# An encoder trunk in split fp32: all high products of a slot ahead of its low products, and the low parts of every fourth MLP tile made elsewhere

## The chip, the cores and the metric

The kernel runs on one NeuronCore of one Trainium2 chip. The metric is the device time of one execution in microseconds (us). Its matmuls run on TensorE (PE in the profile; its weight loads are PEld), element-wise work on VectorE (DVE) and ScalarE (ACT), a few small operations on GpSimd (POOL), and SyncE (SP) issues the transfers.

## The reference, cut to what matters

Two layers work on 256 tokens of width 2048, all in float32. Each layer is a mixer (differential attention, gated linear attention and retention heads behind one input projection and one output projection), followed by a gated MLP with a depthwise convolution of width 3:

```
h = rmsnorm(x, ln1);  x = x + mixer(h) @ w_o            # mixer: h @ w_in, heads, head norms
h = rmsnorm(x, ln2);  u = h @ w_up                       # w_up: 2048 x 11264
u = conv3(u) + conv_b;  a, g = split(u)
x = x + (a * silu(g)) @ w_down                           # w_down: 5632 x 2048
```

The output is a last rmsnorm of x, 256 x 2048.

## The kernel before, in words

A float32 product is made of three products of rounded parts. Each operand is cut into a high part, rounded to the format fp32r that TensorE reads, and a low part, the rest. Then high times high, low times high and high times low are summed in one accumulator, and low times low is dropped.

The weights come as 402 **slots**, in the order in which they are used (`slot_list`): the input projection, the 16 slots of `wo`, and then for each of three chunks of the MLP (14, 15 and 15 column blocks) alternating slots `upg` and `upa`, and 16 slots `down`. Most slots are one tile of 128 x 2048 elements, 1 MB, that is 16 blocks of 128 x 128; a `down` slot has 14 or 15 blocks.

For each slot there are three tiles from one pool of ten (`wts`, 128 x 2048 each): the raw weights that SP loads (`load`, L151), their high part (`split_hi`, L176, one ACT copy that rounds) and their low part (`split_lo`, L184, one DVE subtraction raw minus high). When slot s comes up, the program first gives out `split_hi(s + 3)` and `split_lo(s + 2)`, then the matmuls of slot s, then `load(s + 5)`. The raw tile goes back to the pool when its low part is made. The pool gives out tiles as they were given back, so the next user of a buffer waits for the last reader of its former tile.

The activations lie as tiles of 128 x 512 (`big`): 256 columns high part, 256 columns low part of the same 256 tokens. The slots of the kinds `gv`, `rv` and `dv` take the activations as TensorE's weights (`mm_token`, L222 to L224, three matmuls of 512 columns for a pair of blocks), `ga` has 64 weight columns (L212). All others, 368 slots, go through `mm_feature`: for each block j one matmul of the high weights with all 512 columns (L206), which gives high times high and high times low side by side in one PSUM bank, and one of the low weights with the high 256 columns (L208), which is added to the second half of the bank:

```
for first in ((True, False) if k < n - 1 else (False, True)):
    if first:
        pe.matmul(pt, lhsT=R(hi[:, w]), rhs=R(a), start=k == 0, stop=k == n - 1)
    else:
        pe.matmul(pt[:, T:], lhsT=R(lo[:, w]), rhs=R(a[:, :T]), start=False, stop=False)
```

So a slot is a row of pairs, high then low, and the last pair is turned round.

Behind the matmuls of an `up` slot its bank is read out (`gather`: ACT L229 copies one half, DVE L230 adds the other, L236 multiplies by the norm), convolved (ACT L805, DVE L806 and L807), and for `upg` put through silu (ACT L814). For `upa` it is multiplied by the gate (DVE L817) and cut into parts (ACT L819, DVE L820). A `down` slot adds its bank to the stream x (DVE L894). Every engine works through its own list in the order in which the program gave the work out and waits at each instruction for the semaphores that it needs. POOL has little to do: the power of minus one half in the norms (L320, L358) and some memsets (L254, L466, L467).

Of the kernel before, what the change touches and what calls it, by code (L numbers as in the profile page):

```python
# [14 lines left out]
AF = mybir.ActivationFunctionType  # L15
ALU = mybir.AluOpType
# [4 lines left out]
P = 128  # L21
T = 256
# [30 lines left out]
def slot_list():  # L53

    out = []
    for l in range(DEPTH):
        for kind, i in in_proj_order():
            out.append((l, kind, i, 0, 512 if kind == "ga" else 2048))
        for o in range(KB):
            out.append((l, "wo", o, 0, 2048))  # L60
        j0 = 0
        for c, n in enumerate(CHUNKS):
            for j in range(j0, j0 + n):
                out.append((l, "upg", j, c, 2048))
                out.append((l, "upa", j, c, 2048))
            for o in range(KB):
                out.append((l, "down", o, c, n * P))
            j0 += n
    return out
# [30 lines left out]
def encoder_kernel(ctx: ExitStack, tc: tile.TileContext, wflat, xT, par, con, masks, gate_w, lam_p, rel_bias, decay, out):  # L100
    nc = tc.nc
    pe, act, dve, pool = nc.tensor, nc.scalar, nc.vector, nc.gpsimd
# [30 lines left out]
    def R(ap):  # L133
        return ap.bitcast(F32R)
# [4 lines left out]
    slots = slot_list()  # L139
# [13 lines left out]
    def parts(s):  # L153

        n = slots[s][4]
        if slots[s][1] == "ga":
            h = his[s][:, :1024].rearrange("p (k c) -> p k c", c=64)
            return raws[s][:, :512].rearrange("p (k c) -> p k c", c=32), h[:, :, :32], h[:, :, 32:]
        return raws[s][:, :n], his[s][:, :n], los[s][:, :n] if s in los else None

    def split_piece(s, q):
# [6 lines left out]
        if q == 3:  # L168
            wts.put(raws.pop(s))

    def split_hi(s):
        if s >= NS or s in his:
            return
        his[s] = wts.get()
        raw, hi, _ = parts(s)
        act.activation(R(hi), raw, AF.Copy)  # L176

    def split_lo(s):
        if s >= NS or s not in raws or s not in his:
            return  # L180
        if slots[s][1] != "ga":
            los[s] = wts.get()
        raw, hi, lo = parts(s)
        dve.tensor_sub(R(lo), raw, hi)  # L184
        wts.put(raws.pop(s))

    def done(s):
# [7 lines left out]
    def mm_feature(s, pt, acts, order=None):  # L195

        hi, lo = his[s], los[s]
        n = len(acts)
        for k, j in enumerate(order or range(n)):
            a = acts[j]  # L200
            if k == n // 2 and middle:
                middle.pop()()
            w = slice(j * P, (j + 1) * P)
            for first in ((True, False) if k < n - 1 else (False, True)):
                if first:
                    pe.matmul(pt, lhsT=R(hi[:, w]), rhs=R(a), start=k == 0, stop=k == n - 1)  # L206
                else:
                    pe.matmul(pt[:, T:], lhsT=R(lo[:, w]), rhs=R(a[:, :T]), start=False, stop=False)  # L208

    def mm_ga(s, pt, acts):  # L210
        for k, a in enumerate(acts):
# [653 lines left out]
    first = [banks.get(), banks.get()]  # L865
    for k in range(KB):
        s = k // 4
        norm.operand(k)
        split_piece(s, k % 4)
        mm_token(s, first, norm.acts, [k])  # L870
        if k % 4 == 3:
            done(s)
            load(s + 5)
        if k == 13:
            split_hi(4)
            split_lo(4)
# [52 lines left out]
    for s in range(4, NS + 1):  # L929
# [39 lines left out]
        for t in (1, 2, 3):  # L969
            split_hi(s + t)  # L970
        for t in (1, 2):
            split_lo(s + t)
# [144 lines left out]
```

## Time and profile before

| what | value |
|---|---|
| median of 3 runs | 2334.39 us (2334.32 to 2334.72) |
| the profiled execution's own time | 2334.08 us |
| its span, first to last instruction | 2332.3 us |
| PE busy | 2315.1 us, 99% of the span |
| DVE busy | 1704.8 us, 73% |
| ACT busy | 1231.6 us, 53% |
| POOL busy | 62.3 us, 3% |
| transfers | 423.10 MB, mean 181 GB/s |

Matmuls overlap each other in the pipeline, so the duration of one (398 ns for 512 columns) is longer than the step from its start to the start of the next. What a matmul costs is this step.

### The profile page before, as it was taken

Reading aid. Unit: us, or ns where it says so; the run is one execution under the profiler, and the core shown is the slowest. Engines: PE = TensorE matmul, PEld = TensorE weight load, DVE = VectorE, ACT = ScalarE, POOL = GpSimd, SP = SyncE. Lnnn points to the kernel's source line nnn. Section 1 sums busy time; section 2 is a strip of 40 time slices with the busy share of each in tenths; the row PEclk is TensorE's granted clock in tenths of the full one; section 3 lists DMA queues with packets and bytes.
Section 4 is the critical chain, followed back from the end, with each engine's and each line's share of the span. In section 5 each row is a group of like instructions: output and inputs, shape, how many; then the busy total and the mean of one; then the engine's idle time right before and its main releaser. Section 6 shows DMA issues by size and latency. Waiting matters only on the chain.

```text
span 2332.3 us, 32603 instructions
## 1 busy us (share of the span) xinstructions
PE 2315.1 (99%) x13250; PEld 2004.0 (86%) x13250; DVE 1704.8 (73%) x2459; ACT 1231.6 (53%) x1769; POOL 62.3 (3%) x77
## 2 busy tenths in 40 slices
PE   8999999999999999999999999999999999999998
PEld 7888888888888888888888888888888888888887
DVE  7978886777577765777669789767775777567764
ACT  6557654555345533555445666545543555345553
POOL 0001100000000000000000111000000000000000
PEclk9999999999999999999999999999999999999999
DMA  7444455555555555555554444555545554555552
GB/s 291 167 173 162 161 176 191 180 182 171 196 193 186 190 186 187 191 181 187 185 183 172 145 163 153 193 181 181 187 177 196 185 194 175 187 198 181 186 180 104
DMA packets 66645, 423.10 MB, mean 181 GB/s; under 512 B 7960, under 2 KB 10904, under 8 KB 28096
## 3 DMA queue, kind: packets, MB, share of 16 engines
q1 hardware_dynamic: 66352, 420.96, 51.3%
q8 instruction: 104, 1.70, 0.3%
q14 instruction: 45, 0.37, 0.0%
q10 hardware_dynamic: 144, 0.06, 0.0%
HBM read 417.83 MB, written 2.11 MB: 180 GB/s over the span
## 4 chain that ended last, share of the span: by engine, by line
PE 98%; DVE 2%; DMA 0%; ACT 0%; issue 0%; ACTq 0%; SPq 0%; DVEq 0%
PE bank L206 58%; PE bank L208 29%; PE bank L222 2%; PE bank L223 2%; PE bank L224 2%; PE bank L683 1%; DVE wts L184 0%; PE bank L543 0%; PE bank L265 0%; PE bank L266 0%; DVE big L528 0%; PE bank L212 0%; PE bank L623 0%; PE bank L672 0%; DVE big L568 0%; DMA wts<-wflat 0%
## 5 line engine op out<-in xcount | busy, mean ns | idle before, releaser
L206 PE MATMUL bank<-big,wts 128*128 128x512 f32 x5760 | 2016.8, 398 | 0.0
L208 PE MATMUL bank<-big,wts 128*128 128x256 f32 x5760 | 1556.6, 281 | 0.0
L206 PEld LDWEIGHTS bank<-big,wts 128*128 128x128 f32 x5760 | 1061.4, 188 | 231.6 <-PE bank L591 0.9
L208 PEld LDWEIGHTS bank<-big,wts 128*128 128x128 f32 x5760 | 1087.4, 189 | 32.6
L176 ACT ACTIVATE wts<-wts 128x2048 fp32r<-128x2048 f32 (+3 forms) x398 | 744.1, 1871 | 366.6 <-PE bank L208 348.6
L184 DVE TENSOR_TENSOR wts<-wts,wts 128x2048 fp32r<-128x2048 f32 (+3 forms) x398 | 888.4, 2233 | 12.3 <-PE bank L223 8.2
L894 DVE TENSOR_TENSOR x<-bank,x 128x256 f32<-128x256 f32 x256 | 108.7, 425 | 244.7 <-PE bank L206 240.3
L230 DVE TENSOR_TENSOR sml<-sml,bank 128x256 f32<-128x256 f32 (+1 forms) x242 | 101.6, 420 | 213.6 <-ACT sml L229 213.4
L229 ACT ACTIVATE sml<-bank 128x256 f32<-128x256 f32 (+1 forms) x242 | 92.0, 381 | 168.5 <-PE bank L206 168.2
L819 ACT ACTIVATE big<-sml 128x256 fp32r<-128x256 f32 x88 | 36.8, 418 | 190.5 <-DVE sml L817 190.5
L814 ACT ACTIVATE sml<-sml 128x256 f32<-128x256 f32 x88 | 36.8, 418 | 158.8 <-DVE sml L807 158.8
L222 PE MATMUL bank<-wts,big 128*128 128x512 f32 x256 | 103.0, 402 | 6.0 <-ACT wts L166 6.0
L805 ACT ACTIVATE sml<-sml,conv_t 128x256 f32<-128x256 f32 x176 | 103.8, 590 | 5.7 <-DVE sml L236 5.7
L236 DVE TENSOR_TENSOR sml<-sml,sml 128x256 f32<-128x256 f32 (+1 forms) x230 | 97.8, 425 | 7.9
L223 PE MATMUL bank<-wts,big 128*128 128x512 f32 x256 | 100.8, 394 | 0.0
L224 PE MATMUL bank<-wts,big 128*128 128x512 f32 x256 | 100.5, 393 | 0.0
L806 DVE SCALAR_TENSOR_TENSOR sml<-sml,conv_t,sml 128x255 f32<-128x255 f32 x176 | 84.2, 478 | 8.7 <-ACT sml L805 8.7
L807 DVE SCALAR_TENSOR_TENSOR sml<-sml,conv_t,sml 128x255 f32<-128x255 f32 x176 | 85.2, 484 | 6.3
L820 DVE TENSOR_TENSOR big<-sml,big 128x256 fp32r<-128x256 f32 x88 | 37.4, 425 | 42.6 <-ACT big L819 42.6
L222 PEld LDWEIGHTS bank<-wts,big 128*128 128x128 f32 x256 | 48.6, 190 | 17.2 <-ACT wts L166 6.0
L224 PEld LDWEIGHTS bank<-wts,big 128*128 128x128 f32 x256 | 48.5, 190 | 10.4
L223 PEld LDWEIGHTS bank<-wts,big 128*128 128x128 f32 x256 | 48.6, 190 | 9.8 <-DVE wts L167 0.4
(147 smaller groups left out, 1018.0 us busy)
## 6 DMA issues: line engine op xcount, KB each, us to landing
wts<-wflat SPq DMA_DIRECT2D x300, 1024.0 KB, 4.8
wts<-wflat SPq DMA_DIRECT2D x64, 960.0 KB, 4.7
wts<-wflat SPq DMA_DIRECT2D x32, 896.0 KB, 4.6
wts<-wflat SPq DMA_DIRECT2D x18, 256.0 KB, 5.5
x<-xT SPq DMA_DIRECT2D x8, 256.0 KB, 5.5
out<-big SPq DMA_DIRECT2D x8, 256.0 KB, 3.8
strips<-dr SPq DMA_DIRECT2D x1, 1536.0 KB, 8.6
sml<-sml SPq DMA_DIRECT2D x32, 32.0 KB, 1.9
```

Source lines behind the costliest of these rows:

```text
L176: act.activation(R(hi), raw, AF.Copy)
L184: dve.tensor_sub(R(lo), raw, hi)
L206: pe.matmul(pt, lhsT=R(hi[:, w]), rhs=R(a), start=k == 0, stop=k == n - 1)
L208: pe.matmul(pt[:, T:], lhsT=R(lo[:, w]), rhs=R(a[:, :T]), start=False, stop=False)
L222: pe.matmul(pts[tb], lhsT=al, rhs=R(hi[:, w]), start=k == 0, stop=False)
L223: pe.matmul(pts[tb], lhsT=ah, rhs=R(lo[:, w]), start=False, stop=False)
L224: pe.matmul(pts[tb], lhsT=ah, rhs=R(hi[:, w]), start=False, stop=k == KB - 1)
L229: act.activation(t[:m], pts[0][:m, T:], AF.Copy)
L230: dve.tensor_add(d[:m], t[:m], pts[0][:m, :T])
L236: dve.tensor_mul(d[:m], d[:m], rb[:m])
L805: act.activation(c, us, AF.Identity, scale=w[1], bias=w[3])
L894: dve.tensor_add(xb[i], pts[0][:, h * T:(h + 1) * T], xb[i])
```

## The change

In `mm_feature` the matmuls of one slot are put in another order: first the high weights of all its blocks, then the low weights of all its blocks. Their number and shapes are the same. The matmul that the norm puts into the middle of a slot (`middle`) stays in the middle of the high ones.

Of the MLP's slots (`upg`, `upa`, `down`) those with a number divisible by four get their low part from another engine: 34 slots in each layer, 22 of them `up` and 12 of them `down`. In layer 0 GpSimd subtracts. In layer 1 ACT writes minus the raw tile, rounded, which is minus the high part, and a transfer that GpSimd issues adds the raw tile to it where it lies.

```diff
+    def lo_by(s):
+
+        if slots[s][1] in ("upa", "upg", "down") and s % 4 == 0:
+            return ("pool", "dma")[slots[s][0]]
+        return "dve"
+
...
     def split_lo(s):
         if s >= NS or s not in raws or s not in his:
             return
+        by = lo_by(s)
         if slots[s][1] != "ga":
             los[s] = wts.get()
         raw, hi, lo = parts(s)
-        dve.tensor_sub(R(lo), raw, hi)
+        if by == "dma":
+            act.activation(R(lo), raw, AF.Copy, scale=-1.0)
+            pool.dma_start(R(lo), raw, accum_op=ALU.add)
+        elif by == "pool":
+            pool.tensor_tensor(R(lo), raw, hi, ALU.subtract)
+        else:
+            dve.tensor_sub(R(lo), raw, hi)
         wts.put(raws.pop(s))
...
-            a = acts[j]
             if k == n // 2 and middle:
                 middle.pop()()
-            w = slice(j * P, (j + 1) * P)
-            for first in ((True, False) if k < n - 1 else (False, True)):
-                if first:
-                    pe.matmul(pt, lhsT=R(hi[:, w]), rhs=R(a), start=k == 0, stop=k == n - 1)
-                else:
-                    pe.matmul(pt[:, T:], lhsT=R(lo[:, w]), rhs=R(a[:, :T]), start=False, stop=False)
+            pe.matmul(pt, lhsT=R(hi[:, j * P:(j + 1) * P]), rhs=R(acts[j]), start=k == 0, stop=False)
+        for k, j in enumerate(order or range(n)):
+            pe.matmul(pt[:, T:], lhsT=R(lo[:, j * P:(j + 1) * P]), rhs=R(acts[j][:, :T]), start=False, stop=k == n - 1)
```

PE in layer 1 before, the end of the matmuls of slot 288 (an `upg` slot) and the start of slot 289: `bank` is the accumulator, then come the activations of a block and the weight tile (15276 and 15327 are the high and the low part of slot 288, 15325 and 15379 those of slot 289). What stands in brackets are the semaphores that the instruction waits for, by the engine that raises them (DMAHW: transfers that SP issues, DMASW: transfers that POOL issues).

```order
L206 MATMUL bank_15438<-big_14215,wts_15276 128x512
L208 MATMUL bank_15438<-big_14215,wts_15327 128x256
L206 MATMUL bank_15438<-big_14262,wts_15276 128x512
L208 MATMUL bank_15438<-big_14262,wts_15327 128x256
L208 MATMUL bank_15438<-big_14304,wts_15327 128x256
L206 MATMUL bank_15438<-big_14304,wts_15276 128x512
L206 MATMUL bank_15487<-big_13604,wts_15325 128x512 [waits PE_49,Activation_49]
L208 MATMUL bank_15487<-big_13604,wts_15379 128x256 [waits DVE_49]
L206 MATMUL bank_15487<-big_13651,wts_15325 128x512
L208 MATMUL bank_15487<-big_13651,wts_15379 128x256
```

And now, where the low part of slot 288 is tile 15332 and its high part 15281:

```order
L215 MATMUL bank_15444<-big_14215,wts_15281 128x512
L215 MATMUL bank_15444<-big_14262,wts_15281 128x512
L215 MATMUL bank_15444<-big_14304,wts_15281 128x512
L217 MATMUL bank_15444<-big_13604,wts_15332 128x256 [waits DMASW5_49]
L217 MATMUL bank_15444<-big_13651,wts_15332 128x256
L217 MATMUL bank_15444<-big_13698,wts_15332 128x256
```

The pairs are gone: the 16 low products stand in a row behind the 16 high ones, and the first low product waits for the transfer that made the low tile, where before a low product waited for DVE.

ACT in layer 1 before, about the high part of slot 289 (L176 into 15325): L229 reads out a bank, L805 and L819 belong to the convolution and the gate.

```order
L229 ACTIVATE sml_15321<-bank_15285 128x256 [waits PE_49]
L176 ACTIVATE wts_15325<-wts_15269 128x2048 [waits DMAHW7_49]
L805 ACTIVATE sml_15329<-sml_15320,conv_t 128x256 [waits DVE_49]
L819 ACTIVATE big_15334<-sml_15329 128x256 [waits DVE_49]
L229 ACTIVATE sml_15373<-bank_15337 128x256 [waits PE_49]
L176 ACTIVATE wts_15377<-wts_15318 128x2048 [waits DMAHW0_49]
```

And now:

```order
L238 ACTIVATE sml_15326<-bank_15290 128x256 [waits PE_49]
L182 ACTIVATE wts_15330<-wts_15274 128x2048 [waits DMAHW7_49]
L192 ACTIVATE wts_15332<-wts_15222 128x2048
L814 ACTIVATE sml_15335<-sml_15325,conv_t 128x256 [waits DVE_49]
L828 ACTIVATE big_15340<-sml_15335 128x256 [waits DVE_49]
L238 ACTIVATE sml_15379<-bank_15343 128x256 [waits PE_49]
L182 ACTIVATE wts_15383<-wts_15323 128x2048 [waits DMAHW0_49]
```

A second copy of a whole weight tile (L192, into the low tile of slot 288) stands behind the high part of slot 289 and ahead of the convolution's first step. POOL's transfer onto this tile waits for it.

DVE in layer 0 before, about a slot whose number is divisible by four: L230 and L236 read out a bank, L184 makes a low part (4976 is that slot's), L806 and L807 are the convolution.

```order
L230 TENSOR_TENSOR sml_4969<-sml_4970,bank_4934 128x256 [waits Activation_49]
L236 TENSOR_TENSOR sml_4969<-sml_4969,sml_4180 128x256 [waits DVE_49]
L184 TENSOR_TENSOR wts_4976<-wts_4866,wts_4922 128x2048 [waits DMAHW6_49]
L806 SCALAR_TENSOR_TENSOR sml_4978<-sml_4969,conv_t,sml_4978 128x255 [waits Activation_49]
L807 SCALAR_TENSOR_TENSOR sml_4978<-sml_4969,conv_t,sml_4978 128x255 [waits DVE_49]
L230 TENSOR_TENSOR sml_5018<-sml_5019,bank_4983 128x256 [waits Activation_49]
L236 TENSOR_TENSOR sml_5018<-sml_5018,sml_4180 128x256 [waits DVE_49]
L184 TENSOR_TENSOR wts_5025<-wts_4915,wts_4974 128x2048 [waits DMAHW7_49]
```

And now:

```order
L239 TENSOR_TENSOR sml_4969<-sml_4970,bank_4934 128x256 [waits Activation_49]
L245 TENSOR_TENSOR sml_4969<-sml_4969,sml_4172 128x256 [waits DVE_49]
L815 SCALAR_TENSOR_TENSOR sml_4978<-sml_4969,conv_t,sml_4978 128x255 [waits Activation_49]
L816 SCALAR_TENSOR_TENSOR sml_4978<-sml_4969,conv_t,sml_4978 128x255 [waits DVE_49]
L239 TENSOR_TENSOR sml_5018<-sml_5019,bank_4983 128x256 [waits Activation_49]
L245 TENSOR_TENSOR sml_5018<-sml_5018,sml_4172 128x256 [waits DVE_49]
L197 TENSOR_TENSOR wts_5025<-wts_4915,wts_4974 128x2048 [waits DMAHW7_49,PE_49]
```

The subtraction of tile 4976 has left DVE's list; it is an instruction of POOL now (L195), and the next slot's subtraction (5025) stands where it stood.

## Rows read from the trace of the kernel before

**Rows 1.** The page: busy time of each engine; granted clock of TensorE in 40 slices

```profile
PE 2315.1 (99%) x13250; PEld 2004.0 (86%) x13250; DVE 1704.8 (73%) x2459; ACT 1231.6 (53%) x1769; POOL 62.3 (3%) x77
...
PEclk9999999999999999999999999999999999999999
```

**Rows 2.** The chain that ended last: shares of the span by line

```profile
by line: PE bank L206 57.8%; PE bank L208 29.3%; PE bank L222 2.2%; PE bank L223 2.1%; PE bank L224 2.1%; PE bank L683 0.6%; DVE wts L184 0.5%; PE bank L543 0.5%; PE bank L265 0.4%; PE bank L266 0.4%; DVE big L528 0.3%; PE bank L212 0.3%; P
```

**Rows 3.** Groups by line and shape: xcount | busy us, mean ns | idle before

```profile
L206 PE MATMUL bank<-big,wts 128*128 128x512 f32 x5760 | 2016.8, 398 | 0.0
```

**Rows 4.** The same chain in order of time: start us, us, what

```profile
999.78 0.47 PE bank L206 x2
1000.25 0.11 PE bank L208
1000.36 0.23 PE bank L206
1000.59 0.12 PE bank L208
...
1005.43 0.47 PE bank L206 x2
```

**Rows 5.** Timeline of PE, token slots of 512 columns: start us, us, line, xcount

```profile
12.67 0.39 PE L222 MATMUL bank<-wts,big 128*128 128x512 f32 x1
...
28.99 0.39 PE L222 MATMUL bank<-wts,big 128*128 128x512 f32 x1
...
99.17 0.39 PE L223 MATMUL bank<-wts,big 128*128 128x512 f32 x1
...
100.33 0.39 PE L222 MATMUL bank<-wts,big 128*128 128x512 f32 x1
```

**Rows 6.** Timeline of PE, a run of 256-column matmuls (L265, L266)

```profile
165.66 0.28 PE L265 MATMUL bank<-big,big 128*128 128x256 f32 x1
...
168.52 0.40 PE L206 MATMUL bank<-big,wts 128*128 128x512 f32 x1
```

**Rows 7.** Chain in order of time, the slot with 64 weight columns

```profile
30.51 3.68 PE bank L212 x16
```

**Rows 8.** Timelines of PE and ACT about a slot's end

```profile
1027.88 0.63 PE L206 MATMUL bank<-big,wts 128*128 128x512 f32 x2
...
1028.32 0.38 ACT L229 ACTIVATE sml<-bank 128x256 f32<-128x256 f32 x1 [0.33 <-PE bank L206]
1028.60 1.91 ACT L176 ACTIVATE wts<-wts 128x2048 fp32r<-128x2048 f32 x1
```

**Rows 9.** Timeline of DVE in an up slot

```profile
1023.08 0.42 DVE L230 TENSOR_TENSOR sml<-sml,bank 128x256 f32<-128x256 f32 x1 [1.65 <-ACT sml L229]
1023.53 0.43 DVE L236 TENSOR_TENSOR sml<-sml,sml 128x256 f32<-128x256 f32 x1
1023.88 2.28 DVE L184 TENSOR_TENSOR wts<-wts,wts 128x2048 fp32r<-128x2048 f32 x1
1026.08 0.48 DVE L806 SCALAR_TENSOR_TENSOR sml<-sml,conv_t,sml 128x255 f32<-128x255 f32 x1
1026.59 0.48 DVE L807 SCALAR_TENSOR_TENSOR sml<-sml,conv_t,sml 128x255 f32<-128x255 f32 x1
```

**Rows 10.** Loads: median us from issue to landing; the queue's share of 16 engines (page)

```profile
q1 hardware_dynamic: 66352, 420.96, 51.3%
...
wts<-wflat SPq DMA_DIRECT2D x300, 1024.0 KB, 4.8
```

**Rows 11.** Timelines of DVE and POOL about GpSimd's power in the norms (L358, L320)

```profile
237.63 2.29 DVE L184 TENSOR_TENSOR wts<-wts,wts 128x2048 fp32r<-128x2048 f32 x1
237.87 2.60 POOL L358 TENSOR_TENSOR tny<-tny,mhalf 128x2 f32<-128x2 f32 x1 [18.80 <-DVE tny L357]
...
424.20 0.70 POOL L320 TENSOR_TENSOR tny<-tny,mhalf 128x2 f32<-128x2 f32 x1 [104.25 <-DVE tny L317]
```

**Rows 12.** Groups of POOL: a memset over 512 columns

```profile
L467 POOL MEMSET big<- 128x512 f32 x2 | 1.1, 530 | 0.0
```

## The prediction

> **What bounds the kernel now.** I read the busy times first: PE is busy for 2315.1 us, 99% of the span, and its granted clock stands at the top of the scale in all 40 slices, the higher of its two levels, 2.4 GHz [rows 1]. Next the chain of waits by line: the two lines of the feature slots hold 57.8% and 29.3% of the span, and no other engine comes to one per cent on any line [rows 2]. So whatever makes these matmuls start closer together is time won, and what the other engines do costs nothing until PE has to wait. The 87.1% are 0.871 x 2332.3 = 2031.4 us for 5760 pairs of a high and a low matmul [rows 3], which is 352.7 ns a pair. The chain in order of time shows the pair in its steps: 0.23 us for a high product of 512 columns, 0.11 or 0.12 us for a low one of 256, and 0.47 us for the two high ones that meet where two slots border [rows 4].
>
> **The order of the products.** Nothing is added or removed on PE; the question is what a matmul costs behind one of its own kind. High behind high: the token slots are long rows of 512-column matmuls, each with its own load of 128 weight columns, as the high products will be. Three lines share a row of 72 steps there, from 12.67 to 28.99 us, which is 226.7 ns a step [rows 5]. After a break the row does not start at this pace: five steps from 99.17 to 100.33 take 232 ns each, so I add 5 x 5.3 = 27 ns per slot. Low behind low: 24 steps of 256-column matmuls lie between 165.66 and 168.52, 119.2 ns each [rows 6]. A pair then costs 226.7 + 119.2 = 345.9 ns, and the sum is 5760 x 345.9 = 1992.4 us, plus 368 slots x 27 ns = 9.9 us, 2002.3 us in all. Against 2031.4 us that is 29 us less. I take -29 us.
>
> The bounds, from the nearest rows: the best is 226.7 with the low product's steps of now, 0.115 us as the mean of 0.11 and 0.12 [rows 4], and no slow start: 341.7 x 5760 = 1968.2, -63 us. In the middle is the one slot with 64 weight columns, where 16 matmuls of 512 columns take 3.68 us, 230 ns each [rows 7]; with 119.2 this is 349.2 ns, -20 us. The worst is the two high products at the border, 235 ns each [rows 4]; with 119.2 this is 354.2 ns a pair, +9 us. I take the token slots because they are the longest row with the same shape, and the border pair has a low product just ahead of it, as the first steps of a new row have.
>
> A full slot now takes (1005.43 - 999.78) = 5.65 us [rows 4] and then 16 x 345.9 + 27 = 5.56 us. Can the others follow? DVE has 0.42 + 0.43 + 2.28 + 2 x 0.48 = 4.1 us of work in an `upg` slot [rows 9] and two operations of about 0.43 more in an `upa` slot, 4.95. Both are under 5.56, so DVE does not become the bound.
>
> **GpSimd's low parts, layer 0.** 34 subtractions leave DVE and stand on POOL. No row has a POOL subtraction of 2048 columns. Below: a memset of 512 columns takes 530 ns [rows 12], so one pass over 2048 takes 2.1 us. Above: two reads and a write as three such passes, 6.4 us. I take the upper end. The subtraction can start when the buffer of its output is free, at the end of the slot three before its own, and the low products of its own slot begin after two whole slots and the high row of the third: 2 x 5.56 + 16 x 0.2267 + 0.03 = 14.8 us later. So even 6.4 us is hidden, with 8 us to spare. The raw tile is freed at 6.4 instead of about 3.5 us, and the load that takes its buffer, 4.8 us long [rows 10], ends near 11.2 us; ACT wants it for a high part only at two slots, 11.1 us, and PE at five, 27.8 us. Cost 0; if the cover were gone, 34 x the excess over 14.8 us.
>
> There is a second price: POOL and DVE get in each other's way. GpSimd's power in the norms takes 0.70 us alone, but 2.60 us when it starts under DVE's subtraction of two weight tiles, which runs from 237.63 to 239.92, and it ends 0.55 us after it [rows 11]: POOL stood still until DVE was done. The Trainium skill (SBUF — State Buffer, Who interferes with whom) says that a VectorE instruction with two SBUF inputs and a GpSimd instruction that reads SBUF exclude each other for the whole instruction; the trace agrees for POOL as the one that waits, 2.60 against 0.70 us. So DVE may now stand still while POOL subtracts, and behind its L236 wait the convolution, the next read-out and the next low part. Four `up` slots hold 2 x 4.1 + 2 x 4.95 - 2.28 = 15.8 us of DVE work. DVE's first instruction with two SBUF inputs in a slot is L236 at 1023.53 [rows 9], 1.1 us after the slot's start (1028.12 less 5.65), so up to 5.3 of POOL's 6.4 us block it: 21.1 us, under 4 x 5.56 = 22.2. Cost 0.
>
> **The accumulating transfers, layer 1.** 34 DVE subtractions become an ACT copy and a transfer on POOL's queue each. ACT has room (53% busy [rows 1]). The time that counts is from the copy to the low products. ACT reads out the bank 0.20 us after a slot's first matmul (1028.32; the second high product in the row at 1027.88 starts the slot at 1028.12), makes a high part from 0.48 to 2.39 us, and then the negated copy, of the same length, to about 4.25 us [rows 8]. From there to the low products at 14.8 us are 10.5 us. In the 12 `down` slots no read-out stands ahead of the copy, and 11 to 12 us remain for a somewhat smaller tile.
>
> How long the transfer takes no row shows. Below: like a load, 4.8 us from issue to landing [rows 10]. A load's share of the wire is 51.3% x 2332.3 us x 1.049 MB / 420.96 MB = 3.0 us [rows 10], so 1.8 us are fixed. The accumulation reads two tiles, so 1.8 + 2 x 3.0 = 7.8 us, and one load is on the way beside it in every slot; if half of it falls into the transfer, 9.3 us. Above: two reads and a write that follow each other, with the whole load, 1.8 + 4 x 3.0 = 13.8 us. I take 9.3 us, which is covered with 1.2 us to spare: cost 0. This is the thinnest cover of the change. Past 10.5 us PE stands still at the first low product of each of these slots, with the whole of PE's list behind it; SP's load into the same raw buffer would be late too, but it has until five slots on. DVE and ACT wait for such transfers too where they take over a buffer, mostly one of an earlier slot; a copy that waits on ACT holds the read-outs behind it, which PE misses only when its banks run out. The norm's power of layer 1 stands behind the first transfer on POOL; that is one wait.
>
> **The sum.** Against the execution's own 2334.08 us: -29 + 0 + 0 gives 2305 us. The median of the runs, 2334.39, stands 0.3 us above it, so I keep 2305.
>
> **The rivals.** A, the transfer is late. At 13.8 us PE would wait 3.3 us in 22 `up` slots and about 1 us in 12 `down` slots, 85 us: 2305 + 85 = 2390 us, slower. It decides from 10.5 us on, and eats the whole gain at 10.5 + 29 / 22 = 11.8 us. For it speaks that nothing in the trace shows a transfer that adds, and that the margin is a tenth; against it that only half of the wire is in use. Chance 0.32, a third of it between 10.5 and 11.8 us and so still faster.
>
> B, POOL and DVE block each other longer than I counted. If POOL's subtraction takes 8 us, DVE loses 6.9 us in four slots and needs 22.7 against 22.2: 0.5 us x 22 = 11 us, 2316 us. The long cover to 14.8 us speaks against more. Chance 0.04.
>
> C, the order buys nothing: the high row keeps the border's 235 ns, and the time is between 2334 and 2343 us. For it speaks that a step's length seems to hang on what goes before: the 64-column slot stays at 230 ns and does not settle. [...] Chance 0.12.
>
> The forecast has 0.52. Its own range is 2271 (the best bound) to 2314 us (the 64-column pace). For the range of 8 in 10 I go up to 2400, above A at its price, with one in ten left beyond (a transfer that handles its packets one by one), and down to 2275. About 0.2%, 4.7 us, is what a measurement of this kernel can tell from no change. Faster: the forecast, a third of A and B, less a little where these shade into no change, 0.63. Same: that, and the near end of C, 0.06. Slower: the rest of A and of C, 0.31.
>
> **What would show it.** Right: in the chain of waits steps of 0.227 us in the high rows and 0.12 us in the low rows, up slots of 5.56 us, PE with no idle time before L217, transfers of tile onto tile landing within 10.5 us, and POOL subtractions under 8 us, with the read-out's second instruction on DVE (L236 now, L245 then) as their victim, PE untouched. Wrong: a wait of PE's L217 on a transfer in every fourth slot of layer 1, against none in layer 0, is A; high steps of 235 ns are C; PE waiting for POOL in layer 0 is B.

## The result, and the profile after

| kernel | median of the runs, us | ratio to before, 95% interval |
|---|---|---|
| before, same chip | 2334.55 (2334.32 to 2334.96) | |
| changed | 2401.79 (2398.77 to 2403.34) | 1.0286 [1.0268, 1.0304] |

The changed kernel is slower by 67.2 us, where 2305 us were predicted. The profiled execution has a span of 2399.3 us. The page of the changed kernel, against [rows 1]: busy time, and the two rows of 40 slices for PE and for its granted clock.

```profile
PE 2313.5 (96%) x13250; PEld 2026.9 (84%) x13250; DVE 1663.7 (69%) x2391; ACT 1279.3 (53%) x1803; POOL 258.2 (11%) x145
...
PE   8999999998999989998999999999999898999997
...
PEclk9999999998999989999999999999999999999999
```

PE now has slices below nine tenths, and its share fell from 99% to 96%. The chain of waits by engine (by line it stood in [rows 2] before):

```profile
PE 65%; DVE 18%; DMA 7%; ACT 5%; issue 4%; POOL 1%; ACTq 0%; POOLq 0%; SPq 0%; DVEq 0%
```

Before, the same view gave PE 98% and DVE 2%; now DVE holds 18% and transfers 7%. Yet the matmuls themselves have the pace that was predicted. PE in an undisturbed stretch of layer 0 (start us, us, line, count), against [rows 4 to 6]:

```profile
523.15 3.82 PE L215 MATMUL bank<-big,wts 128*128 128x512 f32 x16
526.80 2.08 PE L217 MATMUL bank<-big,wts 128*128 128x256 f32 x16
528.72 3.82 PE L215 MATMUL bank<-big,wts 128*128 128x512 f32 x16
...
545.42 3.82 PE L215 MATMUL bank<-big,wts 128*128 128x512 f32 x16
```

From start to start the high row takes 3.65 us, 228 ns a step, the low row 1.92 us, 120 ns a step, and the slot 5.57 us; 5.56 were predicted. Over the whole trace the median step is 227 ns behind a high product and 120 ns behind a low one. So the loss is nowhere in the rows. It stands in few places, and the first two of these rows name two kinds of them, while the last two are waits of DVE and ACT (engine, line, what it waited for: us in all, times, longest):

```profile
PE bank L215 <- DVE big L829: 42.4, 9, 8.0
PE bank L217 <- DMA wts<-wts: 19.8, 7, 8.2
DVE wts L197 <- DMA wts<-wts: 92.4, 15, 9.6
ACT big L828 <- DVE sml L826: 249.7, 88, 6.6
```

The first kind is a wait of a high product for the last MLP activation (L829). It falls on the first `down` slot of a chunk, here in layer 0:

```profile
578.82 2.91 PE L215 MATMUL bank<-big,wts 128*128 128x512 f32 x12
585.48 0.50 PE L215 MATMUL bank<-big,wts 128*128 128x512 f32 x1 [3.75 <-DVE big L829]
593.86 0.80 PE L215 MATMUL bank<-big,wts 128*128 128x512 f32 x1 [7.87 <-DVE big L829]
594.45 3.19 PE L217 MATMUL bank<-big,wts 128*128 128x256 f32 x14
597.44 2.91 PE L215 MATMUL bank<-big,wts 128*128 128x512 f32 x7
```

The slot takes 18.6 us from 578.82 to 597.44, where before a slot of 14 blocks took 4.94. The second kind is a wait of a low product for a transfer, in layer 1. Behind either, TensorE's clock is low for a while (the stretches of PE in us from:to, its length, busy time and count of each engine, the granted clock, the DMA share and GB/s; 0.50 is 1.2 GHz, 1.00 is 2.4 GHz):

```profile
1884.70:1888.20 3.50, 3.50 (x18) 2.84 (x16) 1.88 (x5) 2.73 (x4) 0.00 (x0) 1.00 1.02 272
1888.40:1896.60 8.20, 0.12 (x1) 0.00 (x0) 0.00 (x0) 0.05 (x1) 0.00 (x0) 0.81 0.96 268
1896.70:1900.30 3.60, 3.57 (x16) 3.57 (x17) 3.17 (x3) 0.28 (x1) 0.00 (x0) 0.50 0.02 7
```

The 16 low products behind an 8.2 us stall take 3.6 us in place of 1.92.

Of the transfers and of GpSimd the page says this (issues: count, KB each, median us to landing; the queue: packets, MB, share; the group of L195: busy us, mean ns):

```profile
q0 software_dynamic: 4896, 34.61, 7.3%
...
L195 POOL TENSOR_TENSOR wts<-wts,wts 128x2048 fp32r<-128x2048 f32 (+2 forms) x34 | 166.4, 4895 | 599.8 <-ACT wts L182 340.2
...
wts<-wts POOLq DMA_DIRECT2D x22, 1024.0 KB, 8.7
```

Both are inside the bounds of the prediction, 2.1 to 6.4 us and 4.8 to 13.8 us, and below the values taken (6.4 and 9.3).

**The lag.** A number used below is the lag of the last activation: the end of L829 of an `upa` slot, less the start of the next slot on PE. Before, it is 9.4 us at the first slot of layer 0's MLP, falls by 1.2, 1.2 and 1.0 us, and then stays at 5.98 us, but for the last two `upa` slots of a chunk; the last one has 4.54 us. After, in the first chunk of layer 0, it goes 9.3, 12.5, 10.7, 14.0, 12.2, 15.5 and so on to 20.0 us: 1.5 us more with every four slots. Where it comes from is in the rows of POOL and DVE in that stretch:

```profile
521.16 5.70 POOL L195 TENSOR_TENSOR wts<-wts,wts 128x2048 fp32r<-128x2048 f32 x1 [18.07 <-ACT wts L182]
544.93 5.71 POOL L195 TENSOR_TENSOR wts<-wts,wts 128x2048 fp32r<-128x2048 f32 x1 [18.07 <-ACT wts L182]
```
```profile
543.88 2.28 DVE L197 TENSOR_TENSOR wts<-wts,wts 128x2048 fp32r<-128x2048 f32 x1
546.09 4.83 DVE L815 SCALAR_TENSOR_TENSOR sml<-sml,conv_t,sml 128x255 f32<-128x255 f32 x1
550.96 0.48 DVE L816 SCALAR_TENSOR_TENSOR sml<-sml,conv_t,sml 128x255 f32<-128x255 f32 x1
```

POOL's subtraction starts under DVE's low part, and then DVE's convolution step, 0.48 us in [rows 9], lasts 4.83 us, until POOL is done at 550.64. Two subtractions of POOL, four slots apart, lie 23.77 us apart; PE does four slots in 22.27 (523.15 to 545.42 above). The difference is the 1.5 us. Between the two, DVE waits for ACT five times, 3.95 us in all:

```profile
528.61 0.43 DVE L829 TENSOR_TENSOR big<-sml,big 128x256 fp32r<-128x256 f32 x1 [0.48 <-ACT big L828]
...
531.17 0.48 DVE L815 SCALAR_TENSOR_TENSOR sml<-sml,conv_t,sml 128x255 f32<-128x255 f32 x1 [1.35 <-ACT sml L814]
...
532.99 0.42 DVE L239 TENSOR_TENSOR sml<-sml,bank 128x256 f32<-128x256 f32 x1 [0.82 <-ACT sml L238]
...
537.93 0.42 DVE L829 TENSOR_TENSOR big<-sml,big 128x256 fp32r<-128x256 f32 x1 [0.48 <-ACT big L828]
...
543.09 0.42 DVE L239 TENSOR_TENSOR sml<-sml,bank 128x256 f32<-128x256 f32 x1 [0.82 <-ACT sml L238]
```

### The profile page after: what moved, and what is told of

Read it like the earlier page. It is cut to its first block, busy times and chain, and to the rows that moved or that the text cites. A ratio compares the mean times of both kernels' runs of the same rounds, so it can differ in the third digit from the quotient of the medians.

```text
span 2399.3 us, 32990 instructions
## 1 busy us (share of the span) xinstructions
PE 2313.5 (96%) x13250; PEld 2026.9 (84%) x13250; DVE 1663.7 (69%) x2391; ACT 1279.3 (53%) x1803; POOL 258.2 (11%) x145
## 4 chain that ended last, share of the span: by engine, by line
PE 65%; DVE 18%; DMA 7%; ACT 5%; issue 4%; POOL 1%; ACTq 0%; POOLq 0%; SPq 0%; DVEq 0%
PE bank L215 37%; PE bank L217 20%; DVE wts L197 7%; DMA wts<-wts 5%; DVE sml L815 3%; DMA wts<-wflat 2%; PE bank L231 2%; PE bank L232 2%; PE bank L233 2%; DVE sml L816 1%; ACT wts L182 1%; DVE sml L239 1%; POOL tny L367 1%; DVE sml L245 1%; ACT sml L238 1%
## 5 line engine op out<-in xcount | busy, mean ns | idle before, releaser
L215 PE MATMUL bank<-big,wts 128*128 128x512 f32 x5760 | 1392.3, 394 | 43.0 <-DVE big L829 42.4
L215 PEld LDWEIGHTS bank<-big,wts 128*128 128x128 f32 x5760 | 1063.8, 189 | 254.4 <-DVE big L829 46.1
L197 DVE TENSOR_TENSOR wts<-wts,wts 128x2048 fp32r<-128x2048 f32 (+3 forms) x330 | 737.8, 2237 | 126.1 <-DMA wts<-wts 92.4
L217 PEld LDWEIGHTS bank<-big,wts 128*128 128x128 f32 x5760 | 749.2, 194 | 51.9 <-DMA wts<-wts 24.0
L217 PE MATMUL bank<-big,wts 128*128 128x256 f32 x5760 | 759.8, 286 | 19.9 <-DMA wts<-wts 19.8
L195 POOL TENSOR_TENSOR wts<-wts,wts 128x2048 fp32r<-128x2048 f32 (+2 forms) x34 | 166.4, 4895 | 599.8 <-ACT wts L182 340.2
L815 DVE SCALAR_TENSOR_TENSOR sml<-sml,conv_t,sml 128x255 f32<-128x255 f32 x176 | 145.1, 824 | 100.9 <-ACT sml L814 100.9
L239 DVE TENSOR_TENSOR sml<-sml,bank 128x256 f32<-128x256 f32 (+1 forms) x242 | 101.2, 418 | 122.1 <-ACT sml L238 121.7
L193 POOL DMA_DIRECT2D wts<-wts x34 | 29.5, 867 | 831.0 <-ACT wts L192 684.2
L245 DVE TENSOR_TENSOR sml<-sml,sml 128x256 f32<-128x256 f32 (+1 forms) x230 | 105.3, 458 | 7.9
L816 DVE SCALAR_TENSOR_TENSOR sml<-sml,conv_t,sml 128x255 f32<-128x255 f32 x176 | 89.4, 508 | 6.3
L367 POOL TENSOR_TENSOR tny<-tny,mhalf 128x2 f32<-128x2 f32 (+1 forms) x24 | 44.5, 1852 | 445.6 <-DVE tny L366 424.3
L829 DVE TENSOR_TENSOR big<-sml,big 128x256 fp32r<-128x256 f32 x88 | 46.0, 523 | 42.6 <-ACT big L828 42.6
```

The lines of the kernel that those rows point to most:

```text
L195: pool.tensor_tensor(R(lo), raw, hi, ALU.subtract)
L215: pe.matmul(pt, lhsT=R(hi[:, j * P:(j + 1) * P]), rhs=R(acts[j]), start=k == 0, stop=False)
L217: pe.matmul(pt[:, T:], lhsT=R(lo[:, j * P:(j + 1) * P]), rhs=R(acts[j][:, :T]), start=False, stop=k == n - 1)
L239: dve.tensor_add(d[:m], t[:m], pts[0][:m, :T])
L245: dve.tensor_mul(d[:m], d[:m], rb[:m])
L815: dve.scalar_tensor_tensor(c[:, 1:], us[:, :T - 1], w[0], c[:, 1:], ALU.mult, ALU.add)
```

## The experiments

Theory 1: the order gains about 0.09 us a slot; GpSimd sets the chain of DVE and ACT back by keeping DVE from its operands; the bill comes when a chunk's first `down` slot wants the last activation. Theory 2, for layer 1: a transfer holds its raw tile until it has landed, about 8.5 us, another slot's tile takes over that buffer, and DVE, which waits for it, holds up ACT and with it the next transfers. The rivals stand with each run.

**The order alone.** `lo_by` returns "dve" for every slot.

> High products ahead of low ones, every low part back on DVE. Theory 1 (the order gains, the two unloadings lose): undisturbed slots of the changed kernel took 0.087 us less than before, 368 x 0.087 = 32 us; the first down slot of each of six chunks gives back 1.8 us (11 us), since the last MLP activations are now wanted 1.8 us earlier, and a few slots of the mixers give back about 4. So about 2317 us, and the last MLP activation stays within 8 us behind its slot's end in both layers. Rival (it is the new order that makes PE run into late activations, the unloadings only happen beside it): the stalls of 12 to 14 us at the first down slot of a chunk stay, and the time is 2345 us or more.

Measured: 2320.41 us, ratio 0.9941 [0.9925, 0.9958], 13.4 us under before. Undisturbed slots of 16 blocks went from 5.653 to 5.567 us, those of 14 from 4.94 to 4.87. Of the 58 slots of 15 blocks that are not the first of a chunk, half gained 0.08 us and half 0.01; nearly all of the latter took 5.21 or 5.22 us already before. The first `down` slot of each of the six chunks is 1.44 or 1.67 us longer, 9.1 us in all; PE in the same slot as above:

```profile
573.30 3.14 PE L215 MATMUL bank<-big,wts 128*128 128x512 f32 x13
577.90 0.50 PE L215 MATMUL bank<-big,wts 128*128 128x512 f32 x1 [1.46 <-DVE big L829]
578.23 1.84 PE L217 MATMUL bank<-big,wts 128*128 128x256 f32 x14
```

The lag is 5.99 us in both layers, as before. Theory 1 holds; of the stalls that the rival blamed on the order, about a tenth is the order's.

**The order with GpSimd's part, and the order with the transfers.**

```
return ("pool", "dve")[slots[s][0]]     # order_pool
return ("dve", "dma")[slots[s][0]]      # order_dma
```

> The new order with GpSimd's 34 low parts in layer 0, layer 1's low parts all on DVE. Theory 1: the norm's spread and the first down slots of layer 0 cost what they cost in the changed kernel, 6 + 3 x 12 = 42 us above the order alone: about 2359 us, all of it before 1230 us. Rival (a price of the transfers of layer 1 only, or of the order): within 5 us of the order alone.

> The new order with the 34 accumulating transfers of layer 1, layer 0's low parts all on DVE. Theory 1: layer 1 loses what it lost in the changed kernel, 32 us of loss over before plus its 14 us of gain by order less the first slots' price, about 40 us above the order alone: about 2357 us, all of it after 1600 us, at four or five places of 5 to 10 us and not in every fourth slot. Rival (the transfer itself is too slow): a wait of PE at the first low product of nearly every one of the 34 slots.

Measured: 2363.26 us (1.0126 [1.0111, 1.0141]) and 2358.28 us (1.0106 [1.0091, 1.0121]). Against the order alone GpSimd costs 42.9 us and the transfers 37.9, and -13.4 + 42.9 + 37.9 = 67.4 us is the whole of the change's 67.2. With GpSimd the loss is one norm slot (6.5 us, where DVE's spread of the norm, L335, meets POOL's first subtraction: in the changed kernel its two instructions take 4.73 us there, 0.48 under the order alone) and the three first `down` slots with the slot behind each (13.0, 13.1 and 10.8 us); no other slot of layer 0 differs by 0.3 us. With the transfers, three slots hold 7.2, 8.7 and 7.2 us of it, one 3.5 and a few others 0.6 to 1.6 each; most of the 34 slots have no wait. The third of them is a chunk's first `down` slot, where PE waits 6.8 us for the last activation: in layer 1, too, part of the bill is a lag. So it is not the rival, a transfer that is too long everywhere.

**Both parts under the old order.** `mm_feature` as before.

> The old alternating order with both unloadings as in the change. Theory 1: the unloadings cost nearly the same under either order; slots of 5.65 us give the evacuation chain 0.35 us more in four slots and the last activations are wanted 1.8 us later, so the first down slots of layer 0 cost about 8 us instead of 12: 2334 + 6 + 3 x 8 + 37 = about 2400 us. Rival (the unloadings are harmless under the old order, and only the new order's earlier need of high products makes them late): 2334 to 2345 us.

Measured: 2496.22 us, ratio 1.0705 [1.0682, 1.0727]. Theory 1 said about 2400 and the rival 2345 at most: a miss. Slot by slot, the profiled execution (span 2505.1 us) lost only 16.8 us in layer 0 against before, and 155.5 in layer 1. In layer 1 (line L193 of that kernel: who waited for its transfers, us and times):

```profile
  DVE wts L197: 183.8, 28
  PEld bank L221: 126.3, 33
  PE bank L221: 112.1, 32
```

Nearly every transfer is late here: the old order wants the first low product 0.23 us into its slot, the new one behind the high row, 3.65 us into it. That the new order gives the transfers 3.4 us of cover was in none of my sums as a part of its own. In layer 0 the lag grew only in the first chunk (1.16 us per four slots); in the others it rose from 6 or 7.5 us and settled between 8.2 and 10.9, four old slots being 22.61 us long. The two parts of the change are thus not independent of its order, and rival A, a wait of PE at nearly every transfer, came true under the old order.

**GpSimd writes without reading; GpSimd subtracts in quarters.** Both from order_pool; the first leaves the low parts' contribution out:

```
-            pool.tensor_tensor(R(lo), raw, hi, ALU.subtract)
+            for h in range(2):                                   # pool_memset
+                pool.memset(lo, 0.0)
+            for a in range(0, slots[s][4], slots[s][4] // 4):    # pool_quarters
+                c = slice(a, a + slots[s][4] // 4)
+                pool.tensor_tensor(R(lo[:, c]), raw[:, c], hi[:, c], ALU.subtract)
```

> As order_pool (new order, 34 tiles of layer 0 by GpSimd), but GpSimd writes each of these low parts by two memsets of the whole tile and reads nothing (these low parts are zero, their contribution is left out). From a memset of 512 columns at 0.53 us this is about 4.2 us of GpSimd per tile, near the 4.9 us of the subtraction. Theory 1 (the subtraction excludes DVE's instructions with two SBUF operands while it runs): without reading, DVE's convolution steps stay at 0.48 us, the lag of the last MLP activation stays at 6.0 us, and the time is that of the order alone, 2320 us. Rival (any GpSimd access of that length slows DVE, or GpSimd's part simply comes late): 2355 to 2365 us, the lag growing to 15 us and more.

> As order_pool, with GpSimd's subtraction cut into four of a quarter of the tile, about 1.2 us each. Theory 1 (DVE waits for the end of one GpSimd instruction, up to 4.4 us now): a DVE instruction waits at most about 1.2 us, three of them meet GpSimd's pieces in one subtraction, so DVE loses 2 to 3.6 us in four slots instead of 4.4; the lag grows by 0 to 0.8 us per four slots instead of 1.5, and the time is 2322 to 2345 us. Rival (the lock is not handed over between GpSimd's pieces): as order_pool, 2363 us.

Measured: 2321.86 us (0.9950 [0.9933, 0.9967]) and 2322.85 us (0.9952 [0.9937, 0.9967]). DVE's first convolution step in order_pool, pool_memset and pool_quarters, with POOL's rows for the full tiles in the last two (count, busy us, mean ns, idle):

```profile
L815 DVE SCALAR_TENSOR_TENSOR sml<-sml,conv_t,sml 128x255 f32<-128x255 f32 x176 | 145.1, 824 | 33.8 <-ACT sml L814 33.8
```
```profile
L816 DVE SCALAR_TENSOR_TENSOR sml<-sml,conv_t,sml 128x255 f32<-128x255 f32 x176 | 84.5, 480 | 37.7 <-ACT sml L815 37.7
L196 POOL MEMSET wts<- 128x2048 f32 x44 | 79.6, 1809 | 387.4 <-PE bank L216 366.5 <-PE bank L218 19.6
```
```profile
L197 POOL TENSOR_TENSOR wts<-wts,wts 128x512 fp32r<-128x512 f32 x88 | 123.1, 1430 | 350.0 <-PE bank L219 330.8 <-DVE wts L199 19.3
...
L817 DVE SCALAR_TENSOR_TENSOR sml<-sml,conv_t,sml 128x255 f32<-128x255 f32 x176 | 86.4, 491 | 28.3 <-ACT sml L816 28.3
```

Two memsets, 3.6 us a tile, leave DVE at 480 ns and the lag at 5.98 us: what holds DVE is not GpSimd's work but its reading. The Trainium skill (SBUF — State Buffer, Who interferes with whom) says so: a VectorE instruction with two SBUF inputs meets a GpSimd instruction that reads SBUF, not one that only writes it. Here the trace agrees, 824 against 480 ns. So does the read-out's first instruction in order_pool (L239, one operand in a PSUM bank and one in SBUF), which takes 419 ns on the mean, against 420 under the order alone. The quarters take POOL longer in all, 4 x 1.43 = 5.7 us, and yet cost 2.4 us in place of 42.9: the lag falls back to 5.99 us by the tenth `upa` slot and stays there, since a DVE instruction waits for a quarter and not for the whole. The time is near the low end of what was expected.

**GpSimd in every eighth slot.** `s % 8 == 0` in order_pool.

> As order_pool, with GpSimd's part in every eighth slot of layer 0 instead of every fourth (17 tiles, half as many). Theory 1 (each subtraction sets the chain of DVE and ACT back by about 3.6 us, and a slot without one lets it catch up by 0.52 us, as the lag falls at a chunk's start from 9.3 over 8.3 and 7.2 to 6.2 us in two slots each): eight slots give back 4.2 us, so the lag does not grow, and what is left is at most 2 us at each first down slot: 2321 to 2327 us. Rival (a price for each subtraction): half of what order_pool lost, 2341 us.

Measured: 2320.86 us, ratio 0.9944 [0.9928, 0.9961]. This is a little under the expected range. Half of the subtractions cost 0.5 us, not half of 42.9. The lag goes 7.6, 6.5, 6.0, 6.0 in each eight slots of the second and third chunk. The price is one of a chain that does or does not catch up, as theory 1 has it.

**The transfer adds the high part; the copy goes first; the transfer goes one slot early.** All from order_dma, with the edits cut to their lines; the first leaves the low parts' contribution out:

```
-            pool.dma_start(R(lo), raw, accum_op=ALU.add)
+            pool.dma_start(R(lo), R(hi), accum_op=ALU.add)       # dma_from_hi
+        if lo_by(s + 2) == "dma": split_lo(s + 2)                # dma_first: ahead of split_hi(s + 1..3)
+        if lo_by(s + 3) == "dma": split_lo(s + 3)                # dma_early: behind them
```

> As order_dma (new order, 34 transfers in layer 1), but the transfer adds the high part instead of the raw tile, so that the raw tile is free when ACT has read it (these low parts come out as zero, their contribution is left out). Same size, same queue, same issue. Only 3 of 33 low parts of the next slot then stand in the raw buffer of a transfer, instead of 14. Theory 2 (what loses time in layer 1 is DVE waiting with the next slot's low part for the buffer that the transfer still reads, and ACT and the next transfer's issue behind it): DVE's waits for transfers fall from 87 us to under 25, the stalls of 7 to 9 us mostly go, and the time is 2320 to 2332 us. Rival (the transfer's own length or its share of the wire): as order_dma, 2358 us.

> As order_dma, but the negated copy stands ahead of the next high part in ACT's order, so that the transfer is issued 1.9 us earlier in a slot; the buffers fall so that 20 of 33 low parts of the next slot (14 in order_dma) stand in the raw buffer of a transfer. Theory 2 (DVE's wait for that buffer delays ACT and, with it, the next transfers): DVE's waits for transfers stay, 90 us or more in about 20, stalls of several us remain at a chunk's start, and the time is 2350 us or more. Rival (the transfers are late only because they are issued late): the 1.9 us cover most of the stalls, PE waits for transfers under 5 us in all, and the time is 2320 to 2335 us.

> As order_dma, but the negated copy and the transfer are issued one slot earlier (three slots ahead instead of two); nothing left out. The buffers then fall so that 1 of 33 low parts of the next slot stands in a transfer's raw buffer (31 raw tiles pass theirs to the load three slots on). Theory 2: no late issue and no wait of DVE, so PE waits for no transfer and the time is that of the order alone, 2320 us, within 3 us. Rival (the 34 extra transfers slow the loads and each other): 2335 us or more, with ACT's high parts waiting for loads.

Measured: 2352.24 us (1.0079 [1.0064, 1.0094]), 2422.57 us (1.0380 [1.0365, 1.0396]) and 2330.19 us (0.9984 [0.9974, 0.9993]). Line L193 in order_dma, dma_from_hi, dma_first and dma_early: who waited for its transfers (us, times), and the time from issue to landing.

```profile
  DVE wts L197: 87.4, 14
...
  PE bank L217: 20.1, 9
...
DMA to landing us min/median/max: 6.6/8.5/11.9
```
```profile
  PE bank L217: 23.2, 21
...
DMA to landing us min/median/max: 6.7/11.3/12.9
```
```profile
  DVE wts L197: 104.0, 19
...
  PE bank L217: 52.1, 16
  ACT wts L182: 51.4, 9
...
DMA to landing us min/median/max: 6.7/9.8/13.5
```
```profile
  DVE wts L197: 2.2, 1
...
DMA to landing us min/median/max: 6.9/8.5/11.5
```

dma_first speaks for theory 2 against its rival: with the copy first and 20 takeovers in place of 14, it is 64 us slower than order_dma, not faster. It does not price DVE's takeovers alone, since ACT now waits for transfers too (51.4 us in 9 high parts, 3.0 us in one of order_dma) and the next high part stands behind the copy. dma_from_hi agrees in the mechanism and not in the time: DVE's waits for transfers are gone, and so are the stalls of 7 to 9 us, but the time is 20 us over what was expected and only 6 us under order_dma, because now the transfer itself lands in 11.3 us and PE waits a little 21 times, 3.2 us at the most. Its raw tile is free early, so SP's next load runs at the same time: between issue and landing lie 5.2 us of load packets on the mean (over the 16 engines) where order_dma has 2.4, and over the 34 transfers landing time and this load time go together with a correlation of 0.98. The packets of the transfer take 5.05 us in both. So theory 2 and its rival both have a part: the raw tile held back by the transfer keeps the wire clear for it, and costs DVE its buffer. In dma_early 1 of 33 low parts stands in such a buffer and PE waits for no transfer, as theory 2 has it; yet 9.8 us of the order's gain are gone. The profiled execution, 12 us over the order alone, lost most of it in two first `down` slots (4.7 and 6.2 us with the slot behind each). In this run ACT waited 133.3 us in 48 waits for loads, 20.4 us in 8 under the order alone: the rival's mechanism, at a smaller price. Since dma_early changes both the takeovers and the cover, the 28 us that it wins over order_dma are not split between the two.

> As dma_from_hi (the transfer adds the high part, these low parts come out as zero, their contribution is left out), but issued one slot earlier, as in dma_early. The raw tile is free as soon as ACT has read it, so no load is held up, and the transfer has about 5.6 us more. Theory 2 (what dma_from_hi lost is the landing of 11 us against the 10.1 from its issue to the low products; what dma_early lost are loads held up until the transfer has read the raw tile, with ACT's chain and the first down slots behind them): no wait of PE for a transfer, ACT's waits for loads back under 60 us from 133, and the time is that of the order alone, 2320 to 2323 us. Rival (34 more transfers slow the whole machine in some other way): 2328 us or more, as dma_early.

Measured: 2327.01 us, ratio 0.9968 [0.9955, 0.9980], between the two expectations. PE waits for a transfer once, 1.1 us, so the first half of theory 2's reading holds. The second half fell: ACT's waits for loads stayed at 117.5 us though no load is held up by a transfer's reading, and the transfers land after 13.3 us on the median. Here the loads are slowed on the wire: in layer 1's MLP they are issued as early as under the order alone, 1.80 us before the next slot's start on the median, but land after 6.9 us on the mean in place of 4.8. In dma_early the buffers had their part as well: the loads were issued 2.0 us later and landed after 5.9 us. The Trainium skill (DMA: Bandwidth & Descriptors, Issuing engines are not separate DMA queues) says that transfers of all issuing engines run on the same 16 engines and interleave; the 8.5, 11.3 and 13.3 us to landing agree.

**The order, with the last pair held back.** Every low part on DVE; in the first slot of `down` and of `wo` one pair stands behind the rest:

```
cut = n - 1 if slots[s][1] in ("wo", "down") and slots[s][2] == 0 else n
for part in (ks[:cut], ks[cut:]):
    # the high products of the part, then its low products
```

> The new order, every low part on DVE, and in the first slot of each chunk's down products and of wo the last product pair (high and low) stands behind all others, so that the last activation is wanted about as late as under the old order. In the order alone the six first down slots took 1.4 to 1.7 us longer than before (9.1 us in all), the two first wo slots 0.6 us. Theory 1 (these are waits for the last activation and nothing else): 2320.4 - 9 - 1 = about 2310 us, no wait of PE for the last MLP activation. Rival (the first slot is slow for another reason, such as the read-out's bank or the weights): as the order alone, 2320 us.

Measured: 2310.17 us, ratio 0.9899 [0.9884, 0.9914]: 10.2 us under the order alone, as theory 1 has it. PE's list of waits has none for L829's line any more. This is the fastest kernel of the study, 23.5 us under before.

## Why the prediction was wrong, step by step

- **What bounds the kernel: right.** The order alone moved the time by PE's steps, less what the next two points name.
- **The order's pace: right; its sum: too large.** Steps of 226.7 and 119.2 ns were read from other lines; 227 and 120 came. A full slot gained 0.086 us, 0.09 were predicted, one of 14 blocks 0.067, where the same sum gives 0.068. But the sum priced every pair alike, while some slots did not gain: half of those of 15 blocks 0.01 us each, 27 slots of the mixers nothing (0.4 us longer in all), and the two first `wo` slots grew by 0.6 us each. So -29 us became -22.5 before the price of the next point.
- **"Can the others follow?" failed in a small thing.** It asked whether DVE has the time, not when a result is wanted. In a chunk's first `down` slot the last activation ends 4.54 us into the slot, before and under the order alone. The last high product started at 4.71 us (14 blocks) or 5.06 (15) before; in an undisturbed slot it now starts at 2.97 or 3.19. So PE stands there, and these slots are 1.44 or 1.67 us longer. That is 9.1 us, shown by the order alone and given back by order_late. -22.5 + 9.1 = -13.4 us.
- **GpSimd: duration, cover and the block itself were right, the conclusion "Cost 0" was wrong by 42.9 us.** 4.9 us were within the bounds, PE never waited for POOL, and DVE stood for 4.35 us of a subtraction, where up to 5.3 were allowed. The victim was another one: POOL starts about 5.1 us after a slot's start, so the first convolution step is held (L815, 824 ns on the mean against 479 under the order alone) and the read-out's second instruction hardly (L245, 458 against 426). The failed step is "21.1 us, under 4 x 5.56 = 22.2": it added DVE's busy time and the block and set this sum against PE's time. DVE also waits for ACT between its steps (0.48, 0.82 and 1.35 us at a time in the stretch shown, 3.95 us in four slots), and ACT for DVE. With these waits the round of four slots takes 23.77 us, while PE does its four slots in 22.27. Rival B had the mechanism, but set its point at a subtraction of 8 us and its price at 11; PE does not wait in the `up` slots, whose results go to the next free accumulator bank, and the lag is paid at the first `down` slot.
- **Transfers: landing right, "cost 0" wrong by 37.9 us, and not as rival A has it.** In an undisturbed `up` slot the transfer is issued 5.14 us after the start of the slot two before and the weights of its first low product are loaded from 14.56 on: 9.4 us of cover, where I had 10.5 from the end of the copy, with 8.7 us to landing. PE stands for a transfer in 7 of the 34 slots; in the undisturbed `up` slots 0.2 to 1.2 us are to spare. That the landing came so near the 9.3 us taken is in part luck: the transfer holds back the load that would run beside it, and where loads ran freely (dma_from_hi) it took 11.3 us. The step that failed first is the sentence that DVE and ACT take over "mostly" buffers of an earlier slot: 14 of 33 low parts of the very next slot stand in the raw buffer of a transfer that has just been issued. DVE waits, 92.4 us in all; ACT behind it; and the next copy and transfer are late. How much of the 37.9 us is the takeover and how much the thin cover stays open, since no run changes the takeover alone. In layer 1's second chunk (start us, us, engine, line):

```profile
1881.55 1.90 ACT L192 ACTIVATE wts<-wts 128x2048 fp32r<-128x2048 f32 x1
```
```profile
1883.75 0.86 POOL L193 DMA_DIRECT2D wts<-wts  x1 [26.14 <-ACT wts L192]
```
```profile
1896.71 2.29 DVE L197 TENSOR_TENSOR wts<-wts,wts 128x2048 fp32r<-128x2048 f32 x1 [9.58 <-DMA wts<-wts]
```
```profile
1896.73 1.65 PE L217 MATMUL bank<-big,wts 128*128 128x256 f32 x6 [8.21 <-DMA wts<-wts]
```

  The slot began at 1884.71, so this copy ended 9.9 us after the start of the slot two before (1873.6), against 4.8 in a quiet stretch. One landing, at about 1896.7, releases DVE's next low part and PE's low products alike.
- **Not in the prediction at all: the clock behind a stall.** PE is busy for 2313.5 us in the changed kernel and for 2293.1 under the order alone, with the same matmuls. About 20 of the 81 us that the unloadings cost are matmuls at the low clock behind the stalls: PE is busy for 39.3 us at a granted clock of 0.50, against 0.8 us under the order alone. Stalls of 1.5 us, as under the order alone, show none of it (granted clock 1.00 behind them).
- **The chances.** The forecast had 0.52 and slower than before 0.31. The range, 2275 to 2400, ended 1.8 us under the measurement. That it came so near is luck: its upper end was set for rival A, a transfer that is late at nearly every slot, and the loss has another shape and lies in both layers.

What stays open: why the lag holds still between 8.2 and 10.9 us under the old order in two chunks and grows in the first was read from the lags and not tried; and why half of the slots of 15 blocks took 5.21 us already under the old order was not looked into.

## What to carry to other kernels

Where two engines hand work to and fro, set the length of the whole round, waits included, against the time that it has; busy time says nothing of a chain that runs at its limit. A lag that buffers hide is paid at the next place where the last result is wanted, so look there and not at the slots that cause it. When work moves to a transfer, ask for how long it reads its source, and which tile takes over that buffer next.

## What the runs showed of the hardware that was not expected

- A GpSimd subtraction of a tile takes 4.05 to 5.2 us on the mean (1792 to 2048 columns, with what it waits for DVE) and stops a DVE instruction with two operands in SBUF for as long as it runs: 4.83 in place of 0.48 us. Two instructions that read one tile and a scalar per partition (L335) were held as well, 4.73 us in place of 0.48; POOL came first there, and its subtraction took 4.51 us. Cut into four it costs DVE little (491 and 588 ns for the two convolution steps, 479 and 485 without GpSimd).
- A transfer of about 1 MB that adds one tile onto another takes 6.6 us from issue to landing at the least, and 5.05 us of all 16 engines; with loads beside it the medians of the runs are 8.5 to 13.3 us.
- Matmuls of one shape behind each other run at 227 ns (512 columns) and 120 ns (256), and high and low in turn at 235 and 117 ns, which is 353 ns a pair on the mean against 347.
- Behind a stall of 8 us the granted clock is 0.50 for the next 3.6 us; behind one of 1.5 us it stays at 1.00.
